# Column tiles for C's compression, a second engine for scaling u, later squares, and new lengths in the plan of a three-layer attention kernel

## The chip, the cores and the metric

One core of a Trainium2 chip runs the whole program. The metric is the device time of one execution in microseconds. The kernel before took 923.87 us, the median of three runs from 923.19 to 923.9.

## What is computed

256 tokens of width 1024, one sequence, fp32. Five layers follow each other:

- **AB**: two kinds of attention of 8 heads each beside each other (one over a selection of 64 keys, one with a forget gate), output projection, residual;
- **MLP**: `h + square(relu(rms_norm(h) @ w1)) @ w2`, hidden width 4096;
- **C**: attention with 16 heads in two groups and three branches (compressed, selected, window) that are mixed by gates;
- a second **MLP**;
- **D**: differential attention with 16 heads of two maps each and a gate `silu(z)`, after two norms in a row.

The part of C that the change rewrites is the compression of keys and of values (each `x` is 256 tokens, 2 groups, 64 channels):

```python
tok = np.arange(15)[:, None] * 16 + np.arange(32)[None, :]
def compress(x, pe, w1, w2):
    xb = x[:, tok] + pe[None, None, :, None, :]
    xb = transpose(xb, (0, 1, 3, 2, 4)).reshape(b, 15, 2, 32 * 64)
    return gelu(xb @ w1) @ w2          # w1: 2048 x 128, w2: 128 x 64
```

Each of the 15 windows holds 32 tokens; two groups make 30 rows, and `xb @ w1` is a product of 30 x 2048 with 2048 x 128.

## The kernel before

**Weights.** All large weights arrive in loads of up to 512 KB on SyncE's queue (`fetch`, L381) into three raw buffers. Each is rounded to fp32r on ScalarE or VectorE (wH, L418), and VectorE subtracts the rounded from the raw part (wL, L427). Eight such pairs can be held. A projection is done as three fp32r matmuls, high x high, high x low and low x high (`mm3`, L322). TensorE therefore needs, for every operand, H first and L for the third matmul.

**The order of the work.** Nothing is scheduled at run time. `_Weaver` (L153) plays the whole program through once with a cost for every operation and writes each engine's instructions down in the order that results; each engine then runs its list strictly in that order. Generators ("strands") yield operations; a list of operations means that the planner takes the engine that would be done first, with a toll added for VectorE (L275 to L282, set by layer at L1816: 0, 1.8, 1.8, 1.8, 0.3). Strands with a lower priority number go first where several are ready. The costs stand in `_Engine.cost` (L116) for ScalarE, VectorE and GpSimd and in `T` (L325) for TensorE:

```python
if kw.get("op") == ALU.pow:                # GpSimd, L133
    return 1e-3 * (300 + 165 * n)
cost += 0.003 + (4 * max(_free(c[0]), 128) if c[1].dtype == F32 else
        max(_free(c[0]), 256 if c[1].dtype == F32R else 128)) * 0.4167e-3   # L334
```

`T(calls, beside)` divides by `beside` where matmuls run in separate tiles of the array; before, only `scores2` (L680) does so, with two 64-row tiles for the scores of two heads.

**Start of a layer.** `start_layer` (L551) spawns strands for token tiles t = 0 and 1. A `u_strand` (L539) waits for half of h, transposes four 128 x 128 blocks on TensorE, and `split_cols` (L525) scales the four blocks by the norm's gain on ScalarE (one instruction for each block, L529), rounds them to uH and subtracts to uL. Beside it runs `after(t)`, which squares and sums h on ScalarE (`mean_sq`, L512) and takes the inverse square root on GpSimd (`rsqrt`, L519; power with exponent -0.5). The factor is applied only when a projection is read out of PSUM, so TensorE needs u and not the norm. In layer D `after` (L1582) first squares h, waits for u, multiplies h by the final gain, squares again, and combines both norms.

**Layer C.** The first projection (x1, L1320) gives k and v for the compression, whose pairs of tokens are put side by side by `pair_strand` (L1247). `cmp_strand(y)` (L1322, y = 0 for k, 1 for v) adds the position terms into XB (16 blocks j of 30 columns, L1334) and multiplies: 16 fp32 matmuls accumulate into one bank, the weight block of 128 x 128 stationary and XB's 30 columns moving, in groups of four with a planned pause of REST = 1.3 us (L1340 to L1343). Then comes gelu on 30 columns, and the second small matmul. The projections x2, q0 and q1 (`proj`, L563) are at hand for TensorE meanwhile. The outcome is needed by `cmp_att` (L1390).

**Layer D.** For each of four groups of heads `qk_ev` (L1640) reads the accumulated q and k of a token tile: square on ScalarE, sum on VectorE, an 8-wide power on GpSimd (L1650), the product on VectorE (L1653), and four transposes on TensorE (`transp4`, L660).

In the rows "bank" is PSUM, "slot" a 128 x 1024 buffer, "n" a 128 x 512 buffer; L341 and L339 are the lines that issue all matmuls and all transposes, L113 issues most of the rest.

Of the kernel before, what the change touches and what calls it, by code (L numbers as in the profile page):

```python
# [18 lines left out]
P = 128  # L19
# [12 lines left out]
def _constants():  # L32
# [31 lines left out]
    add("pairs", np.concatenate([t == 2 * pair, t == 2 * pair + 1], axis=1))  # L64
    add("sel8", (t % 32 == np.arange(8)[None, :]) & (t < 40))
    add("hblock", (t // 16) == np.arange(8)[None, :])
    return np.ascontiguousarray(np.concatenate(cols, axis=1))
# [34 lines left out]
class _Engine:  # L102
# [13 lines left out]
    def cost(self, name, a, kw):  # L116
# [16 lines left out]
        if kw.get("op") == ALU.pow:  # L133
            return 1e-3 * (300 + 165 * n)
        if name == "tensor_scalar":
# [126 lines left out]
def tile_kernel(ctx: ExitStack, tc: tile.TileContext, I: dict, out: bass.AP):  # L262
# [24 lines left out]
    GAINW = 5.5  # L287
    HALF = 0
    T1W = 0
    LATE = 7  # L290
# [34 lines left out]
    def T(calls, beside=1):  # L325
        late = calls if callable(calls) else lambda: calls
        cost = work = 0.0
        for c in late():
            if len(c) == 3:
                cost += 0.109  # L330
                work += 0.053
            else:
                work += _free(c[0]) * (4 if c[1].dtype == F32 else 1) * c[1].shape[0] / 128 * 0.4167e-3
                cost += 0.003 + (4 * max(_free(c[0]), 128) if c[1].dtype == F32 else max(_free(c[0]), 256 if c[1].dtype == F32R else 128)) * 0.4167e-3  # L334

        def emit():
            for c in late():
                if len(c) == 3:
                    i = pe.transpose(c[0], c[1], ident[:c[2], :c[2]])  # L339
                else:  # L340
                    i = pe.matmul(c[0], lhsT=c[1], rhs=c[2], start=c[3], stop=c[4], skip_group_check=True)  # L341
            return i
        return _Op("T", cost / beside, emit, None, work)

# [119 lines left out]
    uL = cpool.tile([P, 8, S], F32R, name="uL")  # L464
    WARM = 7.0
    warmth = cpool.tile([P, 256], BF16, name="warmth")
# [57 lines left out]

    def split_cols(b, gains, H, L, evs):  # L525
        n = len(gains)
        yield ("acq", "n2")
        u = n2()[:, :n * P]
        te = yield _run(*(act.activation(out=u[:, j * P:(j + 1) * P], in_=b[:, j * P:(j + 1) * P], func=AF.Copy, scale=g)  # L529
                          for j, g in enumerate(gains)))  # L530
        W.give("B", te)
        uv = u.rearrange("p (k q) -> p k q", k=n)
        yield [dve.tensor_copy(H, uv), act.copy(H, uv)]
        te = yield dve.tensor_tensor(out=L, in0=uv, in1=H.bitcast(F32), op=ALU.subtract)
        W.give("n2", te)
        for ev in evs:
            ev.set(te + 0.1)

    def u_strand(t, k0, nk, gap, gev, hev, uev, late):  # L539
        yield ("ev", hev[t][k0 // 4])  # L540
# [7 lines left out]
        q = slice(t * P, (t + 1) * P)  # L548
        yield from split_cols(b, [gap[:, k:k + 1] for k in ks], uH[:, k0:k0 + nk, q], uL[:, k0:k0 + nk, q], uev)

    def start_layer(gap, gev, hev, after, first=4, late=None):  # L551
        uev = [[_Event() for _ in range(8)] for _ in range(2)]
        for t in range(2):
            n = first if t == 0 else 4
            for k in range(0, 8, n):
                W.spawn(u_strand(t, k, n, gap, gev, hev, uev[t][k:k + n], late), t + 0.1 * k)
            W.spawn(after(t), 1.5)
        return uev
# [645 lines left out]
    def layer_c(pl, hin, hout):  # L1204
# [117 lines left out]
        def cmp_strand(y):  # L1322
# [8 lines left out]
            yield ("acq", "n2")  # L1331
            XB = n2()[:, :480].rearrange("p (j g n) -> p j g n", j=16, g=2)
            pv_ = pairs[:, y].rearrange("p g (n j) -> p j g n", j=8)
            for hf in range(2):  # L1334
                yield dve.tensor_tensor(out=XB[:, 8 * hf:8 * hf + 8], in0=pv_[:, :, :, hf:hf + 15],
                                        in1=peT[:, y, 8 * hf:8 * hf + 8].unsqueeze(2).unsqueeze(3).to_broadcast(
                                            [P, 8, 2, 15]), op=ALU.add)
            yield ("acq", "B")
            b = bank()
            for j0 in range(0, 16, 4):  # L1340
                te = yield T([mm(b[:, :30], wc[y][j // 8][:, j % 8, :], XB[:, j, :, :], j == 0, j == 15)
                              for j in range(j0, j0 + 4)])
                yield ("at", te + REST)  # L1343
            W.give("slot", te, 2)
            W.give("n2", te)
            xs, x3, gel = small(30, "gx", 2), small(30, "gy", 2), small(32, "gz", 2)
            te = yield dve.tensor_copy(xs, b[:, :30])
            W.give("B", te)
            yield pool.memset(gel, 0.0)
            yield dve.tensor_tensor(out=x3, in0=xs, in1=xs, op=ALU.mult)  # L1350
# [5 lines left out]
            gv = gel.rearrange("p (g n) -> p g n", g=2)  # L1356
            yield dve.tensor_tensor(out=gv[:, :, 0:15], in0=xs.rearrange("p (g n) -> p g n", g=2),
                                    in1=x3.rearrange("p (g n) -> p g n", g=2), op=ALU.mult)
            if y == 0:
# [495 lines left out]
```

## Time and profile before

| | |
|---|---|
| median of three runs | 923.87 us |
| the profiled execution | 921.53 us |
| its span, first to last instruction | 919.4 us |
| mean granted TensorE clock | 0.998 |
| TensorE / its weight loads | 901.2 us (98%) / 766.9 us (83%) |
| VectorE / ScalarE / GpSimd | 586.6 / 518.2 / 106.4 us (64% / 56% / 12%) |
| DMA | 144.55 MB, mean 157 GB/s |

The busy time of TensorE is the time in which at least one matmul is in flight; matmuls overlap, so a matmul of 0.39 us may be followed by the next 0.23 us after its start. How fast TensorE gets on is read from the starts. A wait shows only as far as no earlier matmul is still in flight. Of the profile's parts the busy times, TensorE's waits, a table by stages, and the timeline are used. In the timeline a row gives the start, the time until the last of its instructions ends, the engine, line and operation, and in brackets the idle time before it and what ended that.

### The profile page before, as it was taken

Reading aid. Unit: us, or ns where it says so; the run is one execution under the profiler, and the core shown is the slowest. Engines: PE = TensorE matmul, PEld = TensorE weight load, DVE = VectorE, ACT = ScalarE, POOL = GpSimd, SP = SyncE. Lnnn points to the kernel's source line nnn. Section 1 sums busy time; section 2 is a strip of 40 time slices with the busy share of each in tenths; the row PEclk is TensorE's granted clock in tenths of the full one; section 3 lists DMA queues with packets and bytes.
Section 4 is the critical chain, followed back from the end, with each engine's and each line's share of the span. In section 5 each row is a group of like instructions: output and inputs, shape, how many; then the busy total and the mean of one; then the engine's idle time right before and its main releaser. Section 6 shows DMA issues by size and latency. Waiting matters only on the chain.

```text
span 919.4 us, 14126 instructions
## 1 busy us (share of the span) xinstructions
PE 901.2 (98%) x5196; PEld 766.9 (83%) x5196; DVE 586.6 (64%) x1230; ACT 518.2 (56%) x1025; POOL 106.4 (12%) x149
## 2 busy tenths in 40 slices
PE   8999999999999999999999999999999999999998
PEld 6778888999999878888789999998877778777786
DVE  5688646544454457766654445444878878697781
ACT  5666858455544564787575544455637545274450
POOL 3520000000000051120000000000310503204000
PEclk9999999999999999999999999999999999999999
DMA  7756134655555474312236665655674545544431
GB/s 233 207 178 211 55 104 164 203 183 187 189 191 190 133 249 143 110 46 70 74 123 196 208 192 179 198 184 161 161 220 130 159 138 160 165 133 159 140 115 46
DMA packets 65124, 144.55 MB, mean 157 GB/s; under 512 B 7214, under 2 KB 9744, under 8 KB 65056
## 3 DMA queue, kind: packets, MB, share of 16 engines
q1 hardware_dynamic: 63632, 140.68, 48.0%
q0 software_dynamic: 1424, 2.98, 1.6%
q8 instruction: 41, 0.67, 0.3%
q14 instruction: 27, 0.22, 0.1%
HBM read 142.59 MB, written 1.05 MB: 156 GB/s over the span
## 4 chain that ended last, share of the span: by engine, by line
PE 86%; DVE 4%; POOL 4%; DMA 3%; ACT 1%; issue 1%; SPq 0%; POOLq 0%; DVEq 0%; ACTq 0%
PE bank L341 81%; PE bank L339 5%; POOL qrs L113 2%; DVE wL L113 2%; DVE n L113 1%; DMA h<-in_x_dram 1%; ACT wH L113 1%; DMA raw<-in_c_w_in_dram 1%; POOL T L113 1%; POOL drn L113 1%; DMA raw<-in_ab_w_in_dram 1%; DVE qss L113 0%; DMA raw<-in_l_w_in_dram 0%; ACT n L113 0%; DVE dss L113 0%
## 5 line engine op out<-in xcount | busy, mean ns | idle before, releaser
L113 DVE TENSOR_TENSOR wL<-raw,wH 128x1024 fp32r<-128x1024 f32 (+2 forms) x262 | 317.8, 1214 | 187.9 <-ACT wH L113 186.2
L113 ACT CAST wH<-raw 128x1024 fp32r<-128x1024 f32 (+2 forms) x226 | 234.8, 1041 | 225.4 <-PE bank L341 181.4
L341 PE MATMUL bank<-wH,slot 128*128 128x512 f32 (+1 forms) x784 | 258.3, 396 | 1.2 <-ACT slot L113 0.6
L341 PE MATMUL bank<-wH,uH 128*128 128x512 f32 (+2 forms) x448 | 182.8, 408 | 0.5 <-ACT uH L113 0.5
L341 PE MATMUL bank<-wH,uL 128*128 128x512 f32 (+2 forms) x448 | 174.9, 390 | 0.0
L341 PE MATMUL bank<-wL,uH 128*128 128x512 f32 (+2 forms) x448 | 174.6, 390 | 0.0
L341 PEld LDWEIGHTS bank<-wH,slot 128*128 128x128 f32 x784 | 147.2, 188 | 32.1 <-issue 1.7
L341 PE MATMUL bank<-wL,slot 128*128 128x512 f32 (+1 forms) x392 | 152.7, 390 | 0.0
L341 PE MATMUL bank<-uH,wL 128*128 128x256 f32 x448 | 127.4, 284 | 0.0
L341 PE MATMUL bank<-uL,wH 128*128 128x256 f32 x448 | 127.0, 284 | 0.0
L341 PE MATMUL bank<-uH,wH 128*128 128x256 f32 x448 | 126.1, 281 | 0.0
L341 PEld LDWEIGHTS bank<-wH,uH 128*128 128x128 f32 x448 | 85.1, 190 | 20.2 <-issue 2.3
L341 PEld LDWEIGHTS bank<-wH,uL 128*128 128x128 f32 x448 | 84.8, 189 | 18.7 <-DVE uL L113 0.4
L341 PEld LDWEIGHTS bank<-wL,uH 128*128 128x128 f32 x448 | 85.2, 190 | 15.0 <-DVE wL L113 0.2
L341 PEld LDWEIGHTS bank<-uH,wH 128*128 128x128 f32 x448 | 85.0, 190 | 0.6
L341 PEld LDWEIGHTS bank<-uL,wH 128*128 128x128 f32 x448 | 84.3, 188 | 0.6
L341 PEld LDWEIGHTS bank<-wL,slot 128*128 128x128 f32 x392 | 73.8, 188 | 13.0
L341 PEld LDWEIGHTS bank<-uH,wL 128*128 128x128 f32 x448 | 84.6, 189 | 0.0
L113 ACT ACTIVATE E<-E,nb 128x128 f32<-128x128 f32 (+1 forms) x160 | 70.8, 447 | 9.7 <-DVE nb L113 9.6
L113 POOL TENSOR_TENSOR qrs<-qss,neghalf 128x8 f32<-128x8 f32 x16 | 36.3, 2272 | 141.6 <-DVE dss L113 110.0
L341 PEld LDWEIGHTS bank<-slot,PT 128*128 128x128 f32 x384 | 48.7, 191 | 3.9 <-issue 0.7
L113 POOL TENSOR_TENSOR r<-ms,neghalf 128x1 f32<-128x1 f32 x6 | 4.0, 668 | 403.3 <-DVE ms L113 403.3
(206 smaller groups left out, 953.4 us busy)
## 6 DMA issues: line engine op xcount, KB each, us to landing
raw<-in_mlp_w_dram SPq DMA_DIRECT2D x128, 512.0 KB, 3.9
raw<-in_l_w_in_dram SPq DMA_DIRECT2D x64, 512.0 KB, 3.8
raw<-in_ab_w_in_dram SPq DMA_DIRECT2D x16, 512.0 KB, 4.1
raw<-in_l_w_out_dram SPq DMA_DIRECT2D x16, 512.0 KB, 3.4
raw<-in_c_w_in_dram SPq DMA_DIRECT2D x12, 512.0 KB, 4.0
raw<-in_ab_w_out_dram SPq DMA_DIRECT2D x8, 512.0 KB, 3.4
raw<-in_c_w_out_dram SPq DMA_DIRECT2D x8, 512.0 KB, 3.5
slot<-in_ab_w_in_dram SPq DMA_DIRECT2D x8, 256.0 KB, 6.2
```

The costliest lines, as they stand in the source:

```text
L113: return _Op(self.key, self.cost(name, a, kw), lambda: f(*a, **kw), bank[0] if bank else None)
L339: i = pe.transpose(c[0], c[1], ident[:c[2], :c[2]])
L341: i = pe.matmul(c[0], lhsT=c[1], rhs=c[2], start=c[3], stop=c[4], skip_group_check=True)
```

## The change

Five edits, some of them in the plan alone:

1. **Compression.** XB becomes 16 blocks of 32 columns, the 16th window of each group zeroed by GpSimd. Its block is now stationary and the weight block moves (128 columns), and the matmuls of four blocks go to the four 32-column tiles of the array; each tile accumulates four blocks into its own 32 partitions of the bank. The four partial sums are copied to SBUF and added, and transposed, by one fp32 matmul with a new constant `sel32`. The pause is gone. Gelu runs on 32 columns, and the memset of its output is gone.
2. **Scaling of u** may go to ScalarE or VectorE, whichever the planner takes; layer AB (the only one with `late`) keeps ScalarE.
3. **Squares.** `after(t)` starts when all of u of that tile stands.
4. **Priority** of the first tile's u strands is -1.5 instead of 0, in layer AB as before.
5. **Lengths in the plan** for powers and for all matmuls, and 0.4 us more for a matmul block in tiles.

```diff
+    add("sel32", t % 32 == np.arange(32)[None, :])
...
         if kw.get("op") == ALU.pow:
-            return 1e-3 * (300 + 165 * n)
+            return 1e-3 * (380 + (175 if n < 8 else 262) * n)
...
+    SWITCH = 0.4
...
-                work += _free(c[0]) * (4 if c[1].dtype == F32 else 1) * c[1].shape[0] / 128 * 0.4167e-3
-                cost += 0.003 + (4 * max(_free(c[0]), 128) if c[1].dtype == F32 else max(_free(c[0]), 256 if c[1].dtype == F32R else 128)) * 0.4167e-3
+                continue
+            n = _free(c[0])
+            work += n * (4 if c[1].dtype == F32 else 1) * c[1].shape[0] / 128 * 0.4167e-3
+            mode = mode or c[1].shape[0] == 64 or _free(c[1]) < P and beside > 1
+            if c[1].dtype == F32:
+                cost += 2 * max(0.112, 0.004 + 2 * n * 0.4167e-3)
+            elif c[1].dtype == F32R:
+                cost += max(0.112, 0.0145 + n * 0.4167e-3)
+            else:
+                cost += max(0.056, 0.003 + n * 0.4167e-3)
+        cost = cost / beside + (SWITCH if mode else 0.0)
...
-    WARM = 7.0
+    WARM, UP = 7.0, -1.5
...
-    def split_cols(b, gains, H, L, evs):
+    def split_cols(b, gains, H, L, evs, scalers=2):
...
-        te = yield _run(*(act.activation(out=u[:, j * P:(j + 1) * P], in_=b[:, j * P:(j + 1) * P], func=AF.Copy, scale=g)
-                          for j, g in enumerate(gains)))
+        cols = [slice(j * P, (j + 1) * P) for j in range(n)]
+        te = yield [_run(*(act.activation(out=u[:, c], in_=b[:, c], func=AF.Copy, scale=g) for c, g in zip(cols, gains))),
+                    _run(*(dve.tensor_scalar(out=u[:, c], in0=b[:, c], scalar1=g, scalar2=None, op0=ALU.mult)
+                           for c, g in zip(cols, gains)))][:scalers]
...
+        def then(t):
+            for e in uev[t]:
+                yield ("ev", e)
+            yield from after(t)
...
-                W.spawn(u_strand(t, k, n, gap, gev, hev, uev[t][k:k + n], late), t + 0.1 * k)
-            W.spawn(after(t), 1.5)
+                W.spawn(u_strand(t, k, n, gap, gev, hev, uev[t][k:k + n], late, 1 if late else 2), (t if t or late else UP) + 0.1 * k)
+            W.spawn(then(t), 1.5)
...
-            XB = n2()[:, :480].rearrange("p (j g n) -> p j g n", j=16, g=2)
+            XB = n2()
+            X4 = XB.rearrange("p (j g n) -> p j g n", j=16, g=2)
+            yield pool.memset(X4[:, :, :, 15:16], 0.0)
...
-            for j0 in range(0, 16, 4):
-                te = yield T([mm(b[:, :30], wc[y][j // 8][:, j % 8, :], XB[:, j, :, :], j == 0, j == 15)
-                              for j in range(j0, j0 + 4)])
-                yield ("at", te + REST)
+
+            te = yield T([mm(b[32 * q:32 * q + 32, :P], XB[:, 32 * (j0 + q):32 * (j0 + q) + 32],
+                             wc[y][(j0 + q) // 8][:, (j0 + q) % 8, :], j0 == 0, j0 == 12)
+                          for j0 in range(0, 16, 4) for q in range(4)], 4)
...
-            te = yield dve.tensor_copy(xs, b[:, :30])
+            yield ("acq", "n2")
+            parts = n2()[:, :P]
+            te = yield [dve.tensor_copy(parts, b[:, :P]), act.copy(parts, b[:, :P])]
             W.give("B", te)
-            yield pool.memset(gel, 0.0)
+            yield ("acq", "B")
+            b = bank()
+            te = yield T([mm(b[:, :32], parts, K("sel32"), True, True)])
+            W.give("n2", te)
+            xs, x3, gel = small(32, "gx", 2), small(32, "gy", 2), small(32, "gz", 2)
+            te = yield dve.tensor_copy(xs, b[:, :32])
```

## Rows read from the trace of the kernel before

**Rows 1.** Busy time of the engines, the first line of the page.

```profile
PE 901.2 (98%) x5196; PEld 766.9 (83%) x5196; DVE 586.6 (64%) x1230; ACT 518.2 (56%) x1025; POOL 106.4 (12%) x149
```

**Rows 2.** TensorE's waits: us in total, times, longest us.

```profile
PE bank L339 <- DVE n L113: 3.4, 8, 0.7
PE bank L341 <- DVE dup L113: 1.8, 1, 1.8
...
PE bank L339 <- ACT n L113: 0.4, 1, 0.4
```

**Rows 3.** Stages: length, busy us of PE, PEld, DVE, ACT, POOL, clock, DMA, GB/s.

```profile
140.00:150.00 10.00, 10.00 (x49) 8.18 (x49) 7.55 (x11) 9.18 (x19) 0.00 (x0) 1.00 0.44 158
...
158.25:330.00 171.75, 171.75 (x1073) 155.37 (x1073) 86.56 (x84) 90.45 (x126) 5.08 (x8) 1.00 0.57 185
...
380.00:447.00 67.00, 65.87 (x450) 57.82 (x450) 48.48 (x194) 52.41 (x170) 6.34 (x12) 1.00 0.19 64
447.00:470.00 23.00, 20.46 (x114) 15.92 (x113) 12.89 (x31) 15.77 (x43) 1.47 (x2) 1.00 0.13 47
...
680.00:850.00 170.00, 167.26 (x857) 133.27 (x856) 138.19 (x338) 89.14 (x198) 36.38 (x18) 1.00 0.51 152
```

**Rows 4.** Timeline of layer C, two bursts of the compression.

```profile
350.12 0.97 PE L341 MATMUL bank<-n,slot 128*128 128x30 f32 x8
...
350.93 0.38 PE L341 MATMUL bank<-wH,uH 128*128 128x304 f32 x1
...
357.60 1.86 PE L341 MATMUL bank<-n,slot 128*128 128x30 f32 x16
359.30 0.47 PE L341 MATMUL bank<-wH,uH 128*128 128x512 f32 x1
359.61 0.39 PE L341 MATMUL bank<-wL,uH 128*128 128x512 f32 x1
359.84 0.39 PE L341 MATMUL bank<-wH,uL 128*128 128x512 f32 x1
```

**Rows 5.** Timeline of layer AB, a score block in two row tiles.

```profile
94.11 0.93 PE L341 MATMUL bank<-slot 64*128 64x128 f32 x8
94.97 0.50 PE L341 MATMUL bank<-wH,uH 128*128 128x512 f32 x1
95.30 0.39 PE L341 MATMUL bank<-wL,uH 128*128 128x512 f32 x1
```

**Rows 6.** Timeline of layer C, GpSimd.

```profile
352.08 0.67 POOL L113 TENSOR_TENSOR T<-n,const 128x32 f32<-128x32 f32 x3 [11.25 <-ACT n L113]
```

**Rows 7.** Timeline of layer D, a power and the transposes behind it.

```profile
727.08 2.48 POOL L113 TENSOR_TENSOR qrs<-qss,neghalf 128x8 f32<-128x8 f32 x1 [4.58 <-DVE qss L113]
...
729.29 0.40 PE L341 MATMUL bank<-wH,uL 128*128 128x512 f32 x1
...
730.40 0.66 PE L339 MATMUL bank<-const,n 128*128 128x128 f32 x4 [0.71 <-DVE n L113]
...
734.03 0.63 PE L339 MATMUL bank<-const,n 128*128 128x128 f32 x4 [0.21 <-DVE n L113]
```

**Rows 8.** Timeline of the start of the second MLP.

```profile
460.67 1.06 ACT L113 ACTIVATE junk<-h 128x1024 bf16<-128x1024 f32 x1 [3.33 <-DVE h L113]
...
461.72 2.15 ACT L113 ACTIVATE n<-bank,gcol 128x128 f32<-128x128 f32 x8
...
464.43 0.50 PE L341 MATMUL bank<-wH,uH 128*128 128x512 f32 x1 [0.51 <-ACT uH L113]
```

**Rows 9.** Timeline of layer C, the gap ahead of the compression.

```profile
341.72 1.05 ACT L113 CAST wH<-raw 128x1024 fp32r<-128x1024 f32 x1 [3.37 <-DMA raw<-in_c_w_in_dram]
...
344.22 0.71 PE L341 MATMUL bank<-const,dup 128*128 128x128 f32 x4 [1.80 <-DVE dup L113]
```

**Rows 10.** The granted clock behind it, by half microseconds (columns as in rows 3).

```profile
345.50:346.00 0.50, 0.50 (x4) 0.50 (x4) 0.50 (x6) 0.47 (x2) 0.00 (x0) 0.50 0.39 106
...
348.00:348.50 0.50, 0.50 (x4) 0.50 (x3) 0.20 (x1) 0.50 (x2) 0.00 (x0) 0.50 0.86 315
```

More of the change, by code (lines that the diff above doesn't have):

```diff
@@ L327, in T @@
         cost = work = 0.0
+        mode = False
         for c in late():
@@ L342, in emit @@
             return i
-        return _Op("T", cost / beside, emit, None, work)
+        return _Op("T", cost, emit, None, work)
     def events(n, m):
@@ L537, in split_cols, with u_strand @@
             ev.set(te + 0.1)
-    def u_strand(t, k0, nk, gap, gev, hev, uev, late):
+    def u_strand(t, k0, nk, gap, gev, hev, uev, late, scalers):
         yield ("ev", hev[t][k0 // 4])
@@ L548, in u_strand @@
         q = slice(t * P, (t + 1) * P)
-        yield from split_cols(b, [gap[:, k:k + 1] for k in ks], uH[:, k0:k0 + nk, q], uL[:, k0:k0 + nk, q], uev)
+        yield from split_cols(b, [gap[:, k:k + 1] for k in ks], uH[:, k0:k0 + nk, q], uL[:, k0:k0 + nk, q], uev, scalers)
     def start_layer(gap, gev, hev, after, first=4, late=None):
         uev = [[_Event() for _ in range(8)] for _ in range(2)]
+        def then(t):
+            for e in uev[t]:
+                yield ("ev", e)
+            yield from after(t)
         for t in range(2):
@@ L1331, in cmp_strand @@
             yield ("acq", "n2")
-            XB = n2()[:, :480].rearrange("p (j g n) -> p j g n", j=16, g=2)
+            XB = n2()
+            X4 = XB.rearrange("p (j g n) -> p j g n", j=16, g=2)
+            yield pool.memset(X4[:, :, :, 15:16], 0.0)
             pv_ = pairs[:, y].rearrange("p g (n j) -> p j g n", j=8)
             for hf in range(2):
-                yield dve.tensor_tensor(out=XB[:, 8 * hf:8 * hf + 8], in0=pv_[:, :, :, hf:hf + 15],
+                yield dve.tensor_tensor(out=X4[:, 8 * hf:8 * hf + 8, :, 0:15], in0=pv_[:, :, :, hf:hf + 15],
                                         in1=peT[:, y, 8 * hf:8 * hf + 8].unsqueeze(2).unsqueeze(3).to_broadcast(
@@ L1339, in cmp_strand @@
             b = bank()
-            for j0 in range(0, 16, 4):
-                te = yield T([mm(b[:, :30], wc[y][j // 8][:, j % 8, :], XB[:, j, :, :], j == 0, j == 15)
-                              for j in range(j0, j0 + 4)])
-                yield ("at", te + REST)
+            te = yield T([mm(b[32 * q:32 * q + 32, :P], XB[:, 32 * (j0 + q):32 * (j0 + q) + 32],
+                             wc[y][(j0 + q) // 8][:, (j0 + q) % 8, :], j0 == 0, j0 == 12)
+                          for j0 in range(0, 16, 4) for q in range(4)], 4)
             W.give("slot", te, 2)
             W.give("n2", te)
-            xs, x3, gel = small(30, "gx", 2), small(30, "gy", 2), small(32, "gz", 2)
-            te = yield dve.tensor_copy(xs, b[:, :30])
+            yield ("acq", "n2")
+            parts = n2()[:, :P]
+            te = yield [dve.tensor_copy(parts, b[:, :P]), act.copy(parts, b[:, :P])]
             W.give("B", te)
-            yield pool.memset(gel, 0.0)
+            yield ("acq", "B")
[4 more added lines that the diff above has]
+            te = yield dve.tensor_copy(xs, b[:, :32])
+            W.give("B", te)
             yield dve.tensor_tensor(out=x3, in0=xs, in1=xs, op=ALU.mult)
@@ L1356, in cmp_strand @@
             gv = gel.rearrange("p (g n) -> p g n", g=2)
-            yield dve.tensor_tensor(out=gv[:, :, 0:15], in0=xs.rearrange("p (g n) -> p g n", g=2),
-                                    in1=x3.rearrange("p (g n) -> p g n", g=2), op=ALU.mult)
+            yield dve.tensor_tensor(out=gel, in0=xs, in1=x3, op=ALU.mult)
             if y == 0:
```

## The prediction

> **What bounds the kernel now.** First the page's busy time: TensorE has work in flight for 901.2 of 919.4 us, VectorE for 64%, ScalarE for 56% [rows 1]. A microsecond off TensorE's own work is therefore one off the span, as long as something else is ready for it; one off another engine counts only where TensorE stands. Then TensorE's waits, which say where it stands: eight waits on VectorE's n, 3.4 us in all, are the largest entry, one wait of 1.8 us on dup the next, and nine waits of 0.4 to 1.8 us each on VectorE, ScalarE or GpSimd make up the rest, DMA and the start aside [rows 2]. The table by stage puts them in place: no idle time from 140 to 150 us, the start of the first MLP layer, nor from 158.25 to 330, in which layer C starts; 2.54 us (23.00 - 20.46) at the end of layer C; 2.74 us from 680 to 850, in layer D [rows 3]. Last the timeline, at each of these places.
>
> **The compression, before.** For k and for v, 16 fp32 matmuls of 30 columns load 128 weight columns each to stream 30. Each is two records. They come as four bursts of 8 records and two of 16 (one of each is shown). The burst at 350.12 holds TensorE until 350.93, 0.81 us; the one at 357.60 until 359.30, 1.70 us, 0.106 a record [rows 4]. The matmul behind a burst is followed after 0.31 us (359.30 to 359.61), the next after the steady 0.23 of that shape (to 359.84), so 0.08 is lost at each of six restarts. Sum: 4 x 0.81 + 2 x 1.70 + 6 x 0.08 = 7.1 us.
>
> **The compression, after.** The operands are swapped: X is stationary in 32 columns, the weights stream with 128, and four matmuls stand in four column tiles. 32 records of 128 columns for each of k and v. No row has a column tile. A record at the 0.106 of [rows 4] gives 3.4 us for 32 one after another and 0.85 for four abreast. The nearest row is the score block, two row tiles of 64: eight records, four of 128 and four of 256 columns, at 0.106 and twice that 4 x 0.106 + 4 x 0.212 = 1.27 us one after another and 0.64 in pairs; it holds TensorE from 94.11 to 94.97, 0.86 us, and the matmul behind it 0.33 instead of 0.23 [rows 5]. So fp32 tiles do run beside each other here, and entering and leaving such a block costs 0.22 + 0.10 = 0.32 us. The adding matmul is two more records, 0.21 us, and a restart of 0.08. For each of k and v: 0.85 + 0.32 + 0.29 = 1.46, together 2.9. I take four abreast, since the nearest row shows its tiles at the full factor. **Gain 4.2 us** (7.1 - 2.9); one after another it is 2 x (3.4 + 0.61) = 8.0, a loss of 0.9. These are the bounds.
> The Trainium skill (TensorEngine Tiling, Key Properties) says that a change of tiling mode drains the engine; the 0.32 us above agree. The Trainium skill (TensorE: Matmul & The Clock Gate, Part 3) gives 2.38 times for three column tiles; carried to four in proportion, an estimate from that page, the gain would be about 3.7 us.
>
> What hangs on it costs nothing: the two copies of the partial sums go to whichever of ScalarE and VectorE is free, and TensorE has the matmuls of the second and third projection to run meanwhile; without that cover each would show a copy of under 0.4 us plus the way there and back, about 1.5 us in all. The memset moves from the 32-wide gel to X's padding, on GpSimd as before; its queue has been empty for 11.25 us when it next works at 352.08 [rows 6], so neither rope nor DMA issues stand ahead of it. 32 more constant columns are 16 KB in a load that the start already makes. The planned pauses of 1.3 us between bursts vanish, but they were filled with other matmuls.
>
> **Other lengths in the plan.** They change no instruction, only the order written into each queue. The 8-wide power of GpSimd was planned at 0.30 + 8 x 0.165 = 1.62 us, and is now at 0.38 + 8 x 0.262 = 2.48; the row shows 2.48 at 727.08, behind it VectorE's product, and TensorE's transposes stand 0.71 us until 730.40 [rows 7]. The last matmul ahead of them started at 729.29, so TensorE was free for the next at 729.52 and lost 0.88: 0.17 more than the wait shows. There are seven such waits in layer D (one of 0.29, and this one with the next, of 0.21, three times; 3.0 us of idle time, 4.2 with the hidden part). The chain from the accumulated q to its transposes was planned at about 4.4 us by the plan's own formulas (power 1.62, square 0.48, sum 0.60, product 0.67, scaling 0.14, and 0.9 for the ways between), 20 matmuls of 0.216; it becomes 5.24 us at 0.228, 23 matmuls. Two and a half more matmuls of 0.233 cover 0.6 us: the long waits keep 0.27, the short ones go. **Gain 0.46 + 3 x (0.61 + 0.37) = 3.4 us**; bounds 0 (VectorE, whose queue holds the product behind weight remainders, is late instead) and 4.2.
>
> Against it: matmuls now count 0.228 instead of 0.216 (512 columns) and 0.121 instead of 0.110 (256), a score block 0.4 more. So about one matmul in 20 fewer stands between a producer and the TensorE instruction that needs it. Where such a wait is already at its limit it grows by up to a matmul of 0.23. There are nine of them [rows 2], at 0.15 each (between none and 0.23): **loss 1.3 us**; bounds 0 and 2.1, and to the other side a gain, should the 1.8 us wait dissolve (a rival below).
>
> **Squares once u stands, u on two engines, higher priority.** At the end of layer C ScalarE first squares h (460.67, 1.06 us), only then scales eight columns of u (461.72, 2.15 us), and TensorE stands 0.51 us for uH until 464.43 [rows 8]. With the squares behind, u's first four columns are scaled by 461.8 (four of eight, 1.08 us) and rounded some 0.6 us later. TensorE could then start its matmuls between the two last pairs of transposes instead of at 464.43. Had VectorE's remainder uL no delay, it would gain 1.5 us; if the residual addition goes ahead of it (0.7 us), 0.9. **Gain 1.2 us.** Scaling on VectorE is offered, but the plan adds a toll of 1.8 us to it at these starts, so I expect ScalarE to be picked and count nothing. At the starts of the first MLP and of C TensorE has no gap [rows 3], so nothing is won there. In D the first square now comes ahead of h times the final gain, on the way to r: up to 1.2 us later, under cover of the first projection, of which 24 matmuls for each token tile (5.6 us at 0.233) stand queued; without cover at most those 1.2 us. The squares now wait for u's remainder; queued behind them on ScalarE are weight roundings, eight buffers ahead, so I count nothing. Layer AB keeps one scaler and its late wait.
>
> **Sum.** -4.2 - 3.4 - 1.2 + 1.3 = -7.5 us. The profiled execution took 921.53 us (span 919.4 and 2.1 around it), which becomes 914.0; the median of the three runs is 2.3 above it, and the same step takes 923.87 to **916.4**.
>
> **Rivals.**
> *As summed*: 916.4, alone 912.5 to 919.5, chance 0.55.
> *The tiles run one after another* (0.12): +0.9 in place of -4.2 gives 921.5. For it: no row has column tiles, and all four share the same rows of the array. Against: the score block's 0.86 where one after another is 1.27 [rows 5]. The Trainium skill (TensorE: Matmul & The Clock Gate, Part 3) has weight loads overlap running matmuls only where the row groups differ, which here they don't; by that rule this rival would be the case.
> *The gap in layer C closes too* (0.15). At 342.4 TensorE stands 1.80 us for dup, whose copy sits on VectorE behind a weight remainder, that behind a rounding at 341.72 that waited 3.37 us for its DMA. Then the granted clock falls to 0.50, the lower level of 1.2 GHz, for six half microseconds (first and last shown), which loses 1.5 us [rows 9, 10]. If the new order puts dup ahead, -3.3 more: 913.1. Against: the load, not the plan, is late.
> *The time won in C is given back at a load* (0.11): TensorE reaches q's weights 4.2 us earlier and stands there for most of it, 3.2 us say: 919.6. For it the 3.37 us of [rows 9]; against it, that rounding was over by 342.8, ahead of both bursts of [rows 4].
> *Slower: the longer lengths uncover the attention chains* (0.07). 64 maps (8, 8, 32 and 16 in A, B, C and D) each send TensorE to wait twice, for the exponentials and for the copied transposes. If all had no slack, one matmul less each would cost 128 x 0.23 = 30 us; it decides from 38 of them, where it eats the 8.8 us won. With half of them: +14.9 - 8.8 = +6.1, 930. Against: from 380 to 447 only 1.13 of 67 us are idle [rows 3], so these chains have slack now.
>
> **Numbers.** A measurement of this kernel tells about 0.2%, 1.85 us, from no change: faster means below 922.0, slower above 925.7. Faster: 0.53 of the first, 0.07 of the serial tiles, 0.15 and 0.08 of the next two: 0.83. Same: 0.02 + 0.05 + 0.03 = 0.10. Slower: 0.07. The range goes from 911.5, where the gap in C closes with the sum's own spread, to 922.5, past the serial tiles; it leaves out the slower case and the ends.
>
> **What would show it.** The compression: no 128x30 records, two blocks of 32 records of 128 columns that hold TensorE about 1.2 us each instead of 3.4. Layer D: waits of the transposes on n down from 3.0 to about 1 us. End of C: eight scalings ahead of the squares and the first matmul of the second MLP near 463. I am wrong if those blocks take 3 us or more, or if new waits of TensorE on E or PT appear by the dozen.

## The result, and the profile after

The changed kernel takes **918.81 us** (median of 4 runs, 917.83 to 919.79) against 923.53 for the kernel before on the same chip (4 runs, 923.1 to 923.9): ratio 0.9949, 95% interval 0.9932 to 0.9966, or 4.7 us with 3.1 to 6.3. The forecast was 7.5 us less. The profiled execution took 918.52 us, its span 916.7.

Three stretches are compared throughout, cut at the first `uH,wH` matmul of 256 columns of either MLP. Up to the first cut both kernels run the same matmul records, so the cuts are sound. The table by stage, first the kernel before, then the changed one (columns as in rows 3):

```profile
0.00:155.51 155.51, 149.72 (x836) 121.35 (x837) 105.95 (x274) 104.75 (x230) 26.80 (x56) 1.00 0.52 162
155.51:476.40 320.89, 315.27 (x1957) 278.63 (x1956) 187.29 (x387) 191.84 (x392) 27.73 (x60) 0.99 0.46 149
476.40:919.40 443.00, 436.25 (x2405) 366.94 (x2403) 293.35 (x571) 221.61 (x403) 51.86 (x33) 1.00 0.52 161
```

```profile
0.00:159.53 159.53, 152.40 (x836) 122.30 (x837) 107.51 (x275) 103.53 (x229) 26.65 (x57) 0.99 0.51 158
159.53:474.22 314.69, 309.85 (x1961) 272.16 (x1960) 186.18 (x386) 191.41 (x394) 31.40 (x60) 1.00 0.47 152
474.22:916.70 442.48, 436.83 (x2405) 366.77 (x2403) 301.31 (x585) 213.20 (x389) 53.19 (x33) 1.00 0.52 162
```

AB lost 4.0 us, first MLP and C won 6.2, second MLP and D won 0.5, which two executions of one instruction list also differ by (see the table of the experiments). That is not the picture of the forecast (0, -5.4, and with all of the counted 1.3 in D, -2.1). TensorE's waits in the changed kernel, against [rows 2] (us in total, times, longest us), say where to look:

```profile
PE bank L350 <- POOL n L114: 3.5, 5, 1.9
...
PE bank L350 <- DVE dup L114: 1.7, 2, 1.1
PE bank L350 <- DVE n L114: 1.6, 2, 0.9
PE bank L352 <- DVE dup L114: 1.3, 1, 1.3
...
PE bank L352 <- ACT uH L114: 1.1, 1, 1.1
```

The eight waits on VectorE's n have become two, but GpSimd's n, 0.7 in one wait before, now heads the list (1.87 of it in AB, the other four waits, 1.65 together, in C), and uH at the start of the second MLP has gone from 0.5 to 1.1. Four entries of the kernel before, all of them waits between 428 and 459 us in C, are gone:

```profile
PE bank L341 <- ACT slot L113: 0.6, 1, 0.6
PE bank L341 <- ACT PT L113: 0.6, 1, 0.6
PE bank L341 <- DVE slot L113: 0.6, 1, 0.6
PE bank L339 <- DVE slot L113: 0.5, 1, 0.5
```

**Compression.** The timeline of C, where [rows 4] stood:

```profile
351.40 1.08 PE L352 MATMUL bank<-slot,n 128*32 128x128 f32 x32
...
352.41 0.60 PE L350 MATMUL bank<-const,dup 128*128 128x128 f32 x2
352.94 1.08 PE L352 MATMUL bank<-slot,n 128*32 128x128 f32 x32
...
353.95 0.41 PE L352 MATMUL bank<-const,n 128*128 128x32 f32 x2
```

From start to next start, 32 records hold TensorE for 1.01 us, twice: 0.032 a record, where a record without tiles takes 0.106 [rows 4]. So about four run abreast, with some 0.16 us left for entering and leaving. Behind the second block and an adding matmul TensorE then stands 0.61 us for dup, a wait that the kernel before doesn't have.

**Start of the second MLP**, against [rows 8]:

```profile
458.75 2.45 PE L350 MATMUL bank<-const,h 128*128 128x128 f32 x16 [0.21 <-DVE h L114]
459.53 2.17 ACT L114 ACTIVATE n<-bank,gcol 128x128 f32<-128x128 f32 x8
...
461.54 1.19 ACT L114 CAST uH<-n 128x512 fp32r<-128x512 f32 x2
...
462.26 0.50 PE L352 MATMUL bank<-wH,uH 128*128 128x512 f32 x1 [1.06 <-ACT uH L114]
```

All 16 transposes now stand in one block ahead of the first matmul, the eight scalings of the first token tile ahead of the squares: TensorE has nothing left to fill the wait with. Before, the transposes came in four groups, at 460.00, 461.19, 462.32 and last here, among the final matmuls of C:

```profile
463.27 0.66 PE L339 MATMUL bank<-const,h 128*128 128x128 f32 x4 [0.35 <-DVE h L113]
```

**Layer D**, in the timeline the start, in the table by stage the window of [rows 3]:

```profile
661.03 0.66 PE L350 MATMUL bank<-const,n 128*128 128x128 f32 x4 [0.92 <-DVE n L114]
...
677.46 0.66 PE L350 MATMUL bank<-const,n 128*128 128x128 f32 x4 [0.71 <-DVE n L114]
```

```profile
680.00:850.00 170.00, 169.98 (x868) 134.83 (x868) 144.71 (x348) 87.14 (x192) 35.59 (x18) 1.00 0.51 154
```

From 680 to 850 the idle time is 0.02 us instead of 2.74, less than the forecast left there, but D's start has two new waits and the whole stretch is only 0.5 us shorter.

### The profile page after: what moved, and what is told of

It is laid out like the page before. It is cut to its first block, busy times and chain, and to the rows that moved or that the text cites. A ratio compares the mean times of both kernels' runs of the same rounds, so it can differ in the third digit from the quotient of the medians.

```text
span 916.7 us, 14167 instructions
## 1 busy us (share of the span) xinstructions
PE 899.1 (98%) x5200; PEld 761.2 (83%) x5200; DVE 595.0 (65%) x1244; ACT 508.1 (55%) x1012; POOL 111.2 (12%) x150
## 4 chain that ended last, share of the span: by engine, by line
PE 84%; issue 4%; DVE 4%; POOL 4%; DMA 2%; ACT 1%; SPq 0%; POOLq 0%; DVEq 0%; ACTq 0%
PE bank L352 79%; PE bank L350 5%; POOL T L114 2%; DVE wL L114 2%; POOL n L114 1%; DMA raw<-in_l_w_in_dram 1%; ACT wH L114 1%; DMA slot<-in_ab_w_in_dram 1%; DMA raw<-in_c_w_in_dram 1%; POOL r L114 0%; DVE wH L114 0%; ACT n L114 0%; DVE n L114 0%; DVE uL L114 0%; DVE slot L114 0%
## 5 line engine op out<-in xcount | busy, mean ns | idle before, releaser
L114 ACT CAST wH<-raw 128x1024 fp32r<-128x1024 f32 (+2 forms) x216 | 224.8, 1042 | 225.1 <-PE bank L352 198.4
L352 PE MATMUL bank<-slot,PT 128*128 128x64 f32 (+1 forms) x384 | 51.1, 274 | 0.0
L114 DVE CAST wH<-raw 128x1024 fp32r<-128x1024 f32 (+1 forms) x46 | 31.5, 684 | 19.3 <-PE bank L352 17.7
```

The lines of the kernel that those rows point to most:

```text
L114: return _Op(self.key, self.cost(name, a, kw), lambda: f(*a, **kw), bank[0] if bank else None)
```

## The experiments

All are measured beside the kernel before (medians 924.16, 923.74 and 923.63 us in the three batches). The stretches are those of the profiled execution, cut as above, with AB cut once more at its 20th matmul of 512 columns: the start up to there takes 15.6 to 18.4 us, in good part by chance of the execution (see e12). "Half clock" counts the spells at the lower level in the clock column, the program's last few microseconds aside; each lost about 1.7 us, half of its length.

| kernel | median us | ratio to before, 95% | start | rest of AB | MLP and C | MLP and D | half clock |
|---|---|---|---|---|---|---|---|
| before | 923.53 | | 15.62 | 139.89 | 320.89 | 443.00 | C |
| the change | 918.81 | 0.9932 to 0.9966 | 15.77 | 143.76 | 314.69 | 442.48 | AB |
| e1 old matmul lengths | 915.14 | 0.9886 to 0.9935 | 18.41 | 141.05 | 314.09 | 438.95 | none |
| e2 old power length | 921.72 | 0.9944 to 0.9983 | 17.14 | 140.50 | 315.59 | 443.87 | none |
| e3 compression alone | 920.88 | 0.9950 to 0.9977 | 17.04 | 140.41 | 317.87 | 443.38 | twice in C |
| e4 tile after tile | 920.00 | 0.9935 to 0.9984 | 17.54 | 140.70 | 316.18 | 442.68 | start |
| e5 power length alone | 919.23 | 0.9926 to 0.9967 | 16.82 | 141.56 | 320.32 | 440.10 | C |
| e6 no 0.4 for a block | 916.81 | 0.9890 to 0.9937 | 16.92 | 141.59 | 315.67 | 442.62 | start, C |
| e7 old u | 920.08 | 0.9941 to 0.9972 | 17.92 | 140.79 | 316.49 | 443.00 | none |
| e8 e1 with slower rope | 911.74 | 0.9843 to 0.9883 | 15.63 | 141.04 | 314.13 | 438.90 | C |
| e9 lengths 5% under old | 909.76 | 0.9826 to 0.9869 | 18.29 | 138.76 | 314.16 | 438.09 | twice at start, C |
| e10 lengths 5% over new | 926.59 | 1.0018 to 1.0043 | 17.69 | 143.59 | 315.11 | 447.91 | none |
| e11 lag before TensorE | 916.93 | 0.9906 to 0.9948 | 17.32 | 141.71 | 315.61 | 440.16 | C |
| e12 the change again | 919.29 (one run) | | 17.47 | 140.77 | 316.04 | 443.22 | C |

The table also says how far single traces agree. The kernel before and e3 have the same instruction lists in AB and in the last stretch: 139.9 and 140.4, 443.0 and 443.4. The change, e12 and e4 have the same lists throughout, but for the order inside e4's two blocks: 140.8 and 140.7 in AB without the half clock, and 442.5, 443.2 and 442.7 at the end. e1 and e8 have the same lists in the last stretch: 438.95 and 438.90. So a difference of up to 0.7 us between two stretches says nothing.

### The compression by itself, and its tiles (e3, e4)

e3 is the kernel before with the compression's part of the diff and nothing else.

> The kernel before with the new compression alone; lengths and u as before (the plan divides the tiled block by 4 by its old formula). Theory 1 (the tiles save TensorE 4 us and the save is kept): AB 155.5, first MLP and C 320.9 - 4 = 317, the rest 443; the whole 919.5. Theory 2 (the save is given back at the next load or copy): first MLP and C above 319.5, the whole above 922.

Measured: 920.88, 3.3 us less than its batch's kernel before, and 317.87 in the stretch with C, 3.0 shorter: between the theories, nearer to the first. The timeline of C:

```profile
352.75 1.08 PE L342 MATMUL bank<-slot,n 128*32 128x128 f32 x32
353.76 0.50 PE L342 MATMUL bank<-wH,uH 128*128 128x512 f32 x1
```

The block holds 1.01 us here too. The table by half microseconds (columns as in rows 3) shows two spells at the lower clock in C, one where [rows 10] had it and one more:

```profile
348.00:348.50 0.50, 0.50 (x4) 0.50 (x3) 0.50 (x1) 0.41 (x2) 0.00 (x0) 0.50 1.03 385
...
457.00:457.50 0.50, 0.50 (x2) 0.41 (x3) 0.00 (x0) 0.00 (x0) 0.00 (x0) 0.50 0.32 74
```

Without the second spell the stretch would be about 4.7 shorter. So the new compression is worth between 3.3 (median) and 4.7 us, give or take the 0.5 by which like stretches differ; the forecast's 4.2 lies inside.

e4 is the change with the order of the 32 matmuls turned, so that neighbours stand in the same tile:

```diff
-                          for j0 in range(0, 16, 4) for q in range(4)], 4)
+                          for q in range(4) for j0 in range(0, 16, 4)], 4)
```

> The change, but the 16 matmuls of a compression ordered by column tile: four in a row for each tile, so that neighbours share a tile. Same work and same result. Theory 1 (neighbours in different tiles run beside each other, neighbours in one tile can't): a block of 32 records holds TensorE about 3.4 us instead of 1.01, the whole +4 to +5 us against the change. Theory 2 (a record of this shape is simply short, whatever its neighbour): the block stays at 1.0 us and the whole at the change's.

Measured: 920.00; the timeline of C:

```profile
349.94 2.46 PE L352 MATMUL bank<-slot,n 128*32 128x128 f32 x32
352.33 0.44 PE L350 MATMUL bank<-const,dup 128*128 128x128 f32 x2
352.70 2.46 PE L352 MATMUL bank<-slot,n 128*32 128x128 f32 x32
355.09 0.41 PE L352 MATMUL bank<-const,n 128*128 128x32 f32 x2
```

2.39 us a block against 1.01, 0.075 a record against 0.032: most of the overlap comes from neighbours in different tiles, as theory 1 has it, but its 3.4 us for the block and its 4 to 5 us for the whole are too much. Of the 2.8 us that two blocks cost more, 1.5 reach the end of C. In the changed kernel TensorE stands 0.61 us for dup behind the blocks, and here it doesn't.

### The power length alone, and all but it (e5, e2)

e5 is the kernel before with one line of the plan changed; e2 is the change with that line as before:

```diff
-            return 1e-3 * (300 + 165 * n)
+            return 1e-3 * (380 + (175 if n < 8 else 262) * n)
```

> The kernel before, with nothing changed but the length that the plan gives to GpSimd's power. Theory 1 (the power length alone is worth what the forecast gave it in D, 3.4 to 4.2 us, and the changed kernel's other lengths take it back): the stretch from the first matmul of the second MLP to the end 439.0 +- 0.8 against 443.0, the waits of the transposes on n in D gone, the stretch up to the first MLP as before, the time 919.8 +- 1.2. Theory 2 (the gain in D needs the rest of the change too, because the power length only moves the waits): that last stretch 441.5 to 443.5 and the time 922 to 924.

> The change, with the power length in the plan as before. Theory 1 (the power length closes the waits of layer D, and only that): the waits of D's transposes on n come back, three pairs of 0.7 and 0.2 us, D 2.6 us longer; AB unchanged at 159.5; the whole 921.4. Theory 2 (the power length moved AB's order): AB near 155.5, D 2.6 longer, the whole about 917.5.

Measured: e5 takes 919.23, 4.5 us less than before, and the last stretch 440.10 instead of 443.00. Theory 1 holds in kind, its 439.0 just misses. Of the eight waits on VectorE's n one of 0.97 us, at D's start, and one of 0.35 are left. By the medians one line of the plan has all but the whole gain of the change; its trace shows 2.9 of the 4.5 us in D, loses 1.2 to 1.7 in AB, and doesn't show where the rest lies. e2 takes 921.72, near theory 1's time, but its waits in D come back as four of 0.7 to 0.8 us and not as three pairs, and its last stretch is 443.87 against 442.5 to 443.2 of the change's list: beside the new matmul lengths the same line brings 0.7 to 1.4 us in D, beside the old ones (e3's 443.38 to e1's 438.95, where u's edits come in too) 4.4. (e2's trace is of an execution of 918.97, near its fastest, so it doesn't show all that the median lost.)

### u, squares and priority as before (e7)

The change with `split_cols`, `u_strand` and `start_layer` as before:

```diff
-            W.spawn(then(t), 1.5)
+            W.spawn(after(t), 1.5)
```

(and one scaler, priority `t + 0.1 * k` throughout).

> The changed kernel with u scaled, prioritised and followed by the squares as before. Theory 1 (these edits are worth at the second MLP's start about what was forecast, 1.2 us, and cost nothing in D): first MLP and layer C 315.9 +- 0.5 against 314.7, the last stretch 442.5 +- 0.5, the time 920.0 +- 1. Theory 2 (squares that wait for u make D's first group late and give back more than they bring): first MLP and layer C 315.9, the last stretch 439 to 441, the time 916 to 918.

Measured: 920.08, 1.3 us over the change, with intervals that overlap. The last stretch is 443.00, so these edits don't make D's start late and theory 2 falls. Theory 1's numbers hold, not its reason: the start of the second MLP is the same without them:

```profile
459.70 2.45 PE L350 MATMUL bank<-const,h 128*128 128x128 f32 x16 [0.20 <-DVE h L114]
...
460.49 2.17 ACT L114 ACTIVATE n<-bank,gcol 128x128 f32<-128x128 f32 x8
...
463.22 0.50 PE L352 MATMUL bank<-wH,uH 128*128 128x512 f32 x1 [1.07 <-ACT uH L114]
```

The scalings stand ahead of the squares here as well. In e3 and in e5, the compression alone and the power length alone, the squares still go first, so it is the new matmul lengths, or the new parts together, that have moved them. e1 below, with the old matmul lengths and u's edits, has the scalings first through these edits: its waits for h and uH there are 0.35 and 0.26 us, against 0.35 and 0.51 before, a gain of 0.25 and not of 1.2. e7's 1.8 us more in the stretch with C come mostly from one place in its timeline, a copy of dup behind GpSimd's late rope, where the change waits 0.61 (and e12, with the change's lists, not at all, so some of this is chance):

```profile
355.70 0.24 POOL L114 TENSOR_TENSOR n<-T,T 128x32 f32<-128x32 f32 x1
355.98 0.23 DVE L114 COPY dup<-n 128x128 f32<-128x128 f32 x1 [0.92 <-POOL n L114]
...
356.27 0.33 PE L350 MATMUL bank<-const,dup 128*128 128x128 f32 x1 [2.67 <-DVE dup L114]
```

### The matmul lengths (e1, e6, e10, e9, e11)

e1 is the change with `T` as before, lengths and 0.4 us for a block alike.

> The change, with the matmul lengths in the plan as before (and no 0.4 us for a block in tiles); power lengths, compression and u as in the change. Theory 1 (the longer matmul lengths put TensorE's transposes of AB ahead of GpSimd's rope, and the gap of 1.87 us with the half clock behind it is their work): layer AB, up to the first matmul of the first MLP's second chunk, goes from 159.5 back to about 155.5 us, the whole to about 915. Theory 2 (the power lengths moved AB's order): AB stays within 1 us of 159.5 and the whole within 1 us of 918.8.

Measured: 915.14, 3.7 us faster than the change. AB up to the first MLP stays at 159.46 with its slow start, so what theory 1 says of AB falls in this trace, as does theory 2's time; the gain is in D, 438.95 against 442.48. No transpose in D waits. So the lengths cost 3.5 us there (4.3 by e12's 443.22). The two waits of the change at D's start are 1.6 of it. Most of the rest is in no list of waits, since a matmul ahead is still in flight: the products with PT, the copied transposes of the exponentials. First the change, then e1, the same place in D:

```profile
758.50 0.40 PE L352 MATMUL bank<-wH,uL 128*128 128x512 f32 x1
758.83 0.94 PE L352 MATMUL bank<-slot,PT 128*128 128x128 f32 x6
```

```profile
756.93 0.40 PE L343 MATMUL bank<-wH,uL 128*128 128x512 f32 x1
757.17 0.83 PE L343 MATMUL bank<-slot,PT 128*128 128x128 f32 x6
```

In the change the block starts 0.33 us behind the matmul ahead instead of 0.24, when the copy of PT is done, and the six records then take 0.11 longer. Ten of the 16 such blocks of D are late like this in the change, in e12 and in e4, 1.5 us in all; in e1, e8 and the kernel before none is.

e6 separates their two parts:

```diff
-    SWITCH = 0.4
+    SWITCH = 0.0
```

> The changed kernel with the plan's added 0.4 us for each block of 64-row or column-tiled matmuls set to 0; the lengths per matmul stay new. Theory 1 (it is the added 0.4 that makes the plan place D's first group late): the stretch from the second MLP to the end falls from 442.5 to 439.5 +- 0.8, the time to 915.5 +- 1.5. Theory 2 (the new lengths per matmul do it, whatever is added for a block): that stretch stays 442 to 443.5, the time 918 to 920.

Measured: the last stretch is 442.62: not the 0.4 but the lengths per matmul take D's time, theory 2 there. The time is 916.81 all the same, not theory 2's, 2.0 under the change with intervals that just overlap, and no stretch shows where; that stays open.

The forecast's idea was that a plan with shorter matmuls puts more of them between a producer and the TensorE instruction that needs it. The trace has 0.232 us for 512 columns where the old plan has 0.216 and the new one 0.228: the old lengths are wrong, and wrong on the side of slack. e9 goes 5% below the old ones (0.206), e10 5% above the new ones (0.239):

```diff
-        return _Op("T", cost / beside, emit, None, work)
+        return _Op("T", 0.95 * cost / beside, emit, None, work)
...
-        return _Op("T", cost, emit, None, work)
+        return _Op("T", 1.05 * cost, emit, None, work)
```

> The changed kernel with the old matmul lengths (915.1) times 0.95 in the plan, 0.206 us for 512 columns where the trace has 0.232. Theory 1 (a plan that takes TensorE for faster than it is puts more matmuls between a producer and the TensorE instruction that needs it, and this slack is what the new lengths took away): no wait of a transpose on n in D, the last stretch 438.5 to 439.5, the time 914 to 916.5. Theory 2 (where waits fall is the luck of one order, not of the direction in which the lengths err): waits of 0.5 to 1.5 us on n come back somewhere, the time 916 to 921.

> The changed kernel with its new matmul lengths times 1.05 in the plan, 0.239 us for 512 columns. Theory 1 (slack): the waits of transposes on n in D grow or become more than the two of 0.92 and 0.71, the last stretch over 442.5, the time 919 to 925. Theory 2 (luck of one order): as likely shorter as longer, 914 to 923, without more waits on n in D.

Measured: 909.76 and 926.59. At 0.206, 0.216, 0.228 and 0.239 us the last stretch takes 438.09, 438.95, 442.48 and 447.91, the program 909.8, 915.1, 918.8 and 926.6. e9 is faster than either theory had it, e10 slower. The order holds at every step (the first, 0.9 us in D, is little more than like traces differ by), with no wait of a transpose on n in D in the first two, two of together 1.63 us in the third and five of 2.7 in the fourth, where three for E join them (TensorE's waits of e10):

```profile
PE bank L350 <- DVE n L114: 2.7, 5, 1.1
...
PE bank L350 <- DVE E L114: 0.8, 3, 0.3
```

The rest of AB has the same ends, 138.8 and 143.6, and no difference between the two in the middle (141.1 and 140.8, e12). Four lengths in order, over 17 us, speak for slack and against the luck of one order. e10 is slower than the kernel before, which is what the rival of uncovered chains spoke of; the change stands 5% of length away from it. e9 is the fastest kernel of all and shows no wait for GpSimd's n in its list any more.

e11 puts the slack where it is meant to be, in the way to TensorE, at the new lengths:

```diff
-           "PP": 0.102, "TT": 0.0}
+           "PP": 0.102, "TT": 0.0, "AT": 0.4, "DT": 0.4, "PT": 0.4}
```

> The changed kernel with its new lengths; in the plan the way from ScalarE, VectorE or GpSimd to TensorE counts 0.4 us instead of 0.1. Theory 1 (slack is all that the old lengths gave D): with the slack put in by hand the two waits on n in D's first group go, the last stretch falls from 442.5 to 439.5 +- 0.8, the time to 915.5 +- 1.5. Theory 2 (it is another order, not slack): that stretch stays over 441.5, the time 917 to 921.

Measured: 916.93 and 440.16, as theory 1 has it. The waits at D's start become 0.20 and 0.63: less, not gone. A fixed 0.3 us gives back 2.3 of the 3.5 us. Short lengths give slack in proportion to the length of the chain; that this makes the difference was not tried.

### AB and GpSimd (e8, e12)

e8 is e1 with longer sums and products for GpSimd in the plan:

```diff
-        return 1e-3 * (147 + (3.1 if name == "tensor_copy" else 2.11) * n)
+        if name == "tensor_copy":
+            return 1e-3 * (147 + 3.1 * n)
+        return 1e-3 * (300 + 2.8 * n)
```

> The changed kernel with the old matmul lengths (915.1), and in the plan GpSimd's sums and products at 0.30 us and 2.8 ns an element, nearer to what the trace shows beside VectorE, in place of 0.147 and 2.11. Theory 1 (the waits of the transposes of q for GpSimd's rope are what the plan still gets wrong): the wait for n from GpSimd before 60 us is under 0.2 (0.46 with the old matmul lengths, 1.87 in the changed kernel), the first stretch 1 us shorter, the time 914.0 +- 1. Theory 2 (every change of length reshuffles the plan, and what the first stretch does is set by where waits happen to land): the wait may go, but others of 0.5 to 1.5 us take its place; the time 914 to 919.

Measured: 911.74, faster than either theory had it. The wait for GpSimd's n before 60 us is gone; one of 0.42 us on VectorE's n stands there instead. The first stretch is 2.8 shorter, but all of that is the start; the rest of AB is the same (141.04 and 141.05), which is theory 2's picture. In the stretch with C it takes the same 314.1 us in spite of a spell at the lower clock that e1 doesn't have, so 1.7 of the gain lie there: TensorE's waits in that stretch add up to 2.9 us instead of 4.5, those for dup 0.44 instead of 1.31. The rest of the 3.4 us between the medians is not found.

e12 is the changed kernel, unaltered.

> The changed kernel unaltered, for a second trace. Theory 1 (of the 4.0 us that the first stretch lost, 1.7 belong to the half clock of that one execution, which came behind a wait of 1.87 us on GpSimd's n, and the rest to that wait and the order): up to the first MLP 157.5 to 159 without a half clock at 52 to 56. Theory 2 (the half clock belongs to the order): it is there again, with 159.5 +- 0.5.

Measured: AB takes 158.24 and has no half clock at 52 us; theory 1. The same instruction list meets another execution. GpSimd's timeline, first in the trace of the change, then in e12:

```profile
50.55 1.31 POOL L114 TENSOR_TENSOR n<-T,T 128x128 f32<-128x128 f32 x1
```

```profile
50.58 0.46 POOL L114 TENSOR_TENSOR n<-T,T 128x128 f32<-128x128 f32 x1
```

The sum that took 1.31 us stood beside a weight remainder on VectorE that ran from 50.22 to 51.55; in e12 that remainder came only at 50.77, since its load was late, and the sum took 0.46. What followed on TensorE in the trace of the change, and the clock behind it, in half microseconds:

```profile
51.92 0.66 PE L350 MATMUL bank<-const,n 128*128 128x128 f32 x4 [1.87 <-POOL n L114]
```

```profile
52.50:53.00 0.50, 0.50 (x5) 0.50 (x6) 0.50 (x3) 0.39 (x1) 0.50 (x2) 0.50 0.63 78
...
55.00:55.50 0.50, 0.50 (x4) 0.40 (x3) 0.50 (x2) 0.50 (x1) 0.00 (x0) 0.50 0.04 8
```

A wait of 1.87 us, then half clock (0.50, the level of 1.2 GHz) until 55.9. Such a wait doesn't always bring it: e7's of 2.67 us, above, is followed by none. In e12 the wait is 0.46 and the clock stays up in AB, but in C it falls instead, at 348 us:

```profile
348.00:348.50 0.50, 0.50 (x4) 0.50 (x3) 0.48 (x2) 0.34 (x2) 0.00 (x0) 0.50 0.94 352
```

The start differs too. TensorE's first projection, in the trace of the change and in e12:

```profile
10.15 0.48 PE L352 MATMUL bank<-wH,uH 128*128 128x512 f32 x1
10.47 0.39 PE L352 MATMUL bank<-wL,uH 128*128 128x512 f32 x1
10.70 0.40 PE L352 MATMUL bank<-wH,uL 128*128 128x512 f32 x1
```

```profile
11.78 0.78 PE L352 MATMUL bank<-wH,uH 128*128 128x512 f32 x1
12.35 0.63 PE L352 MATMUL bank<-wL,uH 128*128 128x512 f32 x1
12.78 0.58 PE L352 MATMUL bank<-wH,uL 128*128 128x512 f32 x1
```

In e12, behind a longer wait for h (2.46 us against 1.59), matmuls start 0.43 us apart instead of 0.23, although the clock column says 1.00 there; the start takes 1.7 us more. All but the kernel before, the change and e8 have such a start or one at the lower clock.

So without the start the change lost 3.9 us in AB in its own trace, of which 1.7 are the half clock. Most of the rest is the longer wait for GpSimd, 1.87 us against 0.46 in e12 (which has 0.65 of other waits behind it). e12 and e4, the same list without the spell, take 140.8 and 140.7, against 139.9 and 140.4 for the order of before (the kernel before and e3): the order itself costs 0.3 to 0.9. With e12, which like the kernel before has one spell in C, the stages read +0.9, -4.9 and +0.2.

## Why the prediction was right or wrong

Direction and range held (918.81 in 911.5 to 922.5); the likeliest number was 2.4 us too low. Step by step:

- **"The compression", gain 4.2: right.** 1.01 us a block is the forecast's 0.85 abreast and 0.16 more, where it had added 0.32; e3 measures 3.3 to 4.7. Rows 5 were the right neighbour, and the rival of tiles one after another is refuted: even with neighbours in the same tile, 32 records take 2.39 us and not 3.4. What was to cost nothing behind it showed 0.61 us of wait for dup in the change's trace, and none in e12. The rule of the Trainium skill (TensorE: Matmul & The Clock Gate, Part 3) that weight loads overlap running matmuls only where the row groups differ was read as making this rival the case, although the prediction also cites 2.38 times for three column tiles from the same part; here all four tiles share all rows and 32 records take 1.01 us, so the measurement decides against that reading.
- **"Other lengths", the power, gain 3.4: right.** Alone 4.5 us by the medians and 2.9 in the last stretch (e5), on either side of the forecast; with the old matmul lengths D's stretch falls by 4.1 (443.00 to 438.95), all but the 4.2 that the working had as its bound, and the short waits went with the long ones. With the new matmul lengths the same line brings only 0.7 to 1.4 there (e2): the two terms of the sum are not independent.
- **"Other lengths", the matmuls, loss 1.3: the step that failed, in size and in place.** It counted nine waits that the trace of before showed (the 1.8 us on dup among them) and let each grow by 0.15. e1 to the change measures 3.7 us, beyond the bound of 2.1. The nine did not grow: four went, uH grew by 0.55, and together they fell from 6.8 to 5.7 us (4.5 in e12). The loss is in chains that had not waited at all: at D's start (0.92 and 0.71 us), in ten late products with PT in D (1.5 us, nearly 0.4 in each of its three later groups, none of it in the list), and in C in three waits for GpSimd's n that e1 doesn't have (1.5), which there make up for what the end of C wins. That is in part what the rival "the longer lengths uncover the attention chains" spoke of. A row of waits shows where slack has run out and says nothing of how little is left elsewhere.
- **"Squares once u stands", gain 1.2: not shown.** The scalings did go ahead of the squares and the first matmul did come at 462.26, but e7 has the same order without these edits, and the wait grew from 0.51 to 1.06 us: the transposes that were to fill it all stand ahead of it. Where the edits do make the order (e1), the waits there fall by 0.25. That VectorE's scaling would not be picked was right.
- **The rivals.** The gap in C closed in part: dup waits 1.29 us instead of 1.80 and the half clock behind it was absent, but e12 has it again behind 1.4 us of wait. The 6.2 us of that stretch are therefore 4.5 plus one absent spell, and 4.9 in e12, against the forecast's 5.4. Nothing in C was given back at a load.
- **Nothing foresaw AB**, where the change moves no work and the order still costs 0.3 to 0.9 us: new lengths reorder every layer, also those that a diff doesn't touch.
- **Some luck.** The miss of 2.4 us equals what the matmul lengths cost beyond their 1.3, but only because the others cancel: a power worth up to 1.1 more, squares worth little or nothing, AB.

## What to carry to other kernels

In a statically ordered kernel a planner's lengths are also its safety margin: here, nearly true lengths for the bottleneck engine left its instructions standing right behind their producers, and a producer that was late stopped it. Correct the lengths of the engines that are waited for (the power: one line, 4.5 us by the medians), and leave the engine that must not wait somewhat too short in the plan, or add the margin as lag; try the dose on both sides. A stage whose only known cost is a wait list should be costed by how close its chains run, not by the waits that happen to show.

## What the runs showed of the hardware

- Four fp32 column tiles that share all 128 rows run beside each other when neighbours are in different tiles (0.032 us a record of 128 columns, entering and leaving included); with neighbours in the same tile a record takes 0.075, still under the 0.106 of a record without tiles [rows 4]. Why 0.075 was not tried.
- GpSimd's sum of 128x128 takes 0.46 us when it starts ahead of VectorE's subtraction of two SBUF operands, and 1.31 us when it starts inside one; it then ends 0.31 us after VectorE does. (So does, in the same trace, a product that starts at 48.48 and takes 1.20.) That is the exclusive lock of the Trainium skill (SBUF — State Buffer, "SBUF: two separate sides"): one of the two engines holds the shared ports for its whole instruction. The trace agrees.
- A spell at the lower clock lost 1.7 us each time, and the same kernel had it in AB in one execution and in C in the next; the start of a trace differed by 1.7 us between two executions of one kernel, by up to 2.8 over all. Two stretches of single traces may differ by that for no reason in the code: count the spells and cut off the start before comparing, and then trust no difference under 0.7 us.
